# The first three products of a two-request layer on the scaled x, with the share of the norm's shift added as one column for each request

## The chip, the cores and the metric

One core of a Trainium2 chip runs the whole kernel. The metric is the device time of one execution in microseconds (us); lower is better. Profiles are of one execution, and times in a profile count from the start of its span.

## The reference

One layer of a diffusion backbone is computed for two requests with shared weights: 128 context tokens (request 0) and 512 latent tokens (request 1), 640 in all, of width 1024. What matters here is its start:

```
sh1, sc1, g1, sh2, sc2, g2 = split(silu(c) @ w_mod + b_mod, 6)    # one set for each request
h  = rmsnorm(x, norm_g[0]) * (1 + sc1) + sh1
z  = h @ w_in                       # 1024 x 7200
zx, zg, q, k, v, g, lr, ga, gb = split(z)
xc = conv_centred(zx, conv_w, conv_b)          # per row of the grid, for request 1
hf, hb = rg_lru_scan(xc, ...)                  # forward and backward
```

After that come the gated linear attention, two gated up-projections, `w_out`, a second norm and a squared-ReLU MLP. With `a1 = norm_g[0] * (1 + sc1)` the first norm's output is `xn * a1 + sh1`, where `xn` is x divided by its root mean square, and so `h @ w = (xn * a1) @ w + sh1 @ w`. The last term is the same for all tokens of a request.

## The kernel before

Activations lie transposed, features on the 128 partitions and the 640 tokens along the free axis, as 8 tiles of 128 features (k = 0 to 7). A product of h with a weight is made exact enough by splitting both operands into a rounded high part and a low part: weight pieces are `whi` and `wlo`, h is `HH` and `HL`, and each k gives three terms (whi x HH, whi x HL, wlo x HH), each in two halves of 320 tokens. So one output piece of 128 features (a unit) takes 8 x 3 x 2 = 48 matmuls.

**The order of the work.** All operations go into a recorder in program order (`Recorder.add`, with their dependences). `Recorder.order` then simulates the engines with costs of its own and, whenever an engine is free, takes the operation with the lowest index that is ready by its simulation (casts of weights count as 50 places earlier). Each engine issues its own list in that order and does not pass over a waiting instruction. Tiles come from pools: 43 tiles `t` in SBUF, 4 `whi` and 4 `wlo`, 2 raw weight buffers, and in PSUM 2 `dense` and 2 `aux` tiles. A tile is given out of turn only if the tiles that are due before it can still be had. All instructions are issued on line 343, so the profile's groups are told apart by their tiles.

**The start.** The SP queue loads x, and `EARLY` and `MIX` give the order of the rest: `m` in `EARLY` and `l` in `MIX` are loads of `w_mod` (`mod_load`, four DMAs of 256 KB for 256 columns, scale and shift columns in turn, 8 loads in all), `d` and `D` loads of `w_in`, `x` the transposes of a tile of x, `p` the splits of the first weight pieces, `m` in `MIX` a pair (`mod_pair`) and `h` two tiles of h (`make_h`).

`mod_pair(n)` multiplies silu(c) with the scale and the shift columns of tiles 2n and 2n+1. Each product has 32 output rows (two are used), and four of them write four groups of 32 partitions of one `aux` tile. ACT copies the result to `rw`, and products with `sel` add the four groups and turn them into columns, which DVE writes to `a1` and `sh1`. `make_h(k)` scales and shifts tile k (DVE does request 0, ACT request 1), DVE rounds it into `HH` and subtracts for `HL`.

**The first unit.** `first_part(k)` makes tile k of the first three pieces of zx at once (`first_ps`: two `dense`, one `aux`), as soon as `HH` and `HL` of that k are there. `first_post` then calls `post_zx` for each: DVE copies request 0 and ACT request 1 out of PSUM to a padded tile `zp`, and both compute the convolution, from which the LRU chains start (gates on `aux` tiles, tanh, exp, sqrt, scans). The fourth piece, zx3, needs a `dense` tile again, and the units of zx, lr, q, k, v, g and zg follow, all on `HH` and `HL`.

Of the kernel before, what the change touches and what calls it, by code (L numbers as in the profile page):

```python
# [21 lines left out]
GR = 8  # L22
# [15 lines left out]
MH_ENG = "VAVV"  # L38
# [4 lines left out]

EARLY = "xxxrxxmm"
MIX = "XdllxxxxxDllmphllmhmhmh"
N_FIRST = 3


# [341 lines left out]
def tile_hybrid_layer(  # L392
# [8 lines left out]
    V, A, PE, G, SP = (Port(rec, e) for e in ("DVE", "ACT", "PE", "POOL", "SP"))  # L401
# [25 lines left out]
    def flat(ps):  # L427
        return ps.rearrange("p a b -> p (a b)")
# [7 lines left out]
    f32 = lambda ap: ap.bitcast(F32)  # L436
    act = A.activation
    by = {"A": A, "V": V, "G": G}

    def copy(e, dst, src):  # L440
        A.copy(dst, src) if e == "A" else by[e].tensor_copy(dst, src)

    def scaled(e, dst, src, scale, bias):

        if e == "A":
            act(dst, src, AF.Copy if bias is None else AF.Identity, scale=scale, **({} if bias is None else {"bias": bias}))
        else:
            by[e].tensor_scalar(dst, src, scale, bias, op0=OP.mult, **({} if bias is None else {"op1": OP.add}))
# [43 lines left out]
    wm = w_mod[0]  # L492
    wm_r = wm.rearrange("(k p) n -> p k n", p=128)

    def mod_load(m):

        c0 = D * (1 - m % 2) + 256 * (m // 2)
        parts = [t_("modw")[:, 0:512].rearrange("p (k n) -> p k n", k=2) for _ in range(4)]
        for i, p in enumerate(parts):
            SP.dma_start(out=p, in_=wm_r[:, 2 * i:2 * i + 2, c0:c0 + 256])  # L500
        return parts

    def x_load(t):
        a, b = t_(f"xa{t}"), t_(f"xb{t}")
# [2 lines left out]
        SP.dma_start(out=b[:, 0:512], in_=src[..., 512:1024])  # L507
        xin.append((a, b))

    xin, modw = [], []  # L510
    for s_ in EARLY:
        if s_ == "r":
            load_rows(rows_mod, SP)
        elif s_ == "m":
            modw.append(mod_load(len(modw)))
        else:
            x_load(len(xin))


    ps = aux()  # L520
# [17 lines left out]
    cst32 = consts.tile([128, 8, 32], F32, name="cst32")  # L538
# [3 lines left out]
    ps = aux()  # L542
# [6 lines left out]
    sel = consts.tile([128, 2], F32, name="sel")  # L549
# [68 lines left out]
    cols = {}  # L618
    for nm in ("a1", "sh1", "a2", "sh2"):
        cols[nm] = consts.tile([128, 2, 8], F32, name=nm)  # L620
    bm1 = consts.tile([128, 8], F32, name="bm1")
# [7 lines left out]
        for e, x in zip(XN_ENG, xin[t]):  # L629
            scaled(e, x[:, 0:512], x[:, 0:512], q, None)  # L630

    def mod_pair(n):


        ps = aux()

        for m in (1, 0):
            for r in (1, 0):
                for j in (3, 2, 1, 0):
                    k = 4 * r + j  # L640
                    PE.matmul(ps[32 * j:32 * (j + 1), m, 0:256], cst32[:, k, :], modw[2 * n + m][k // 2][:, k % 2, :],
                              start=r == 1, stop=r == 0)
        rw = t_("rw")
        A.copy(rw[:, 0:512].rearrange("p (m c) -> p m c", m=2), ps[:, :, 0:256])
        for m in range(2):
            for i in range(2):
                k = 2 * n + i
                pc = ps[:, m, 256 + 2 * i:258 + 2 * i]
                PE.matmul(pc, rw[:, 256 * m + 128 * i:256 * m + 128 * (i + 1)], sel, start=True, stop=True)
                if m:  # L650
                    V.tensor_scalar(cols["sh1"][:, :, k], pc, bm(0, k), None, op0=OP.add)
                else:
                    V.tensor_scalar(cols["a1"][:, :, k], pc, bm1[:, k:k + 1], ng(0, k), op0=OP.add, op1=OP.mult)

    xnT = []
    HH = rec.tile(big, 1, [128, 8, T], F32R, "HH", "hh")
    HL = rec.tile(big, 1, [128, 8, T], F32R, "HL", "hl")

    def x_T(t, ps):
        for k in range(KT):  # L660
            PE.transpose(flat(ps)[:, 128 * k:128 * (k + 1)], xin[t][k // 4][:, 128 * (k % 4):128 * (k % 4 + 1)], ident)
        for k in range(KT):
            copy(XT_ENG[t], xnT[k][:, 128 * t:128 * (t + 1)], flat(ps)[:, 128 * k:128 * (k + 1)])

    def make_h(k):
# [42 lines left out]
    def startup():  # L708
        ps = aux()
        PE.transpose(ps[:, 0, 0:80], v2[0:80, :], ident[0:80, 0:80])  # L710
        V.tensor_copy(C2, ps[:, 0, 0:80])
        V.tensor_scalar(bm1, bmv(1), 1.0, None, op0=OP.add)
        for t in range(NT):
            x_norm(t)
        load_rows(rows_etc, G)
        ps = aux()
        PE.transpose(ps[:, 0, 0:114], v1[0:114, :], ident[0:114, 0:114])
        V.tensor_copy(C1, ps[:, 0, 0:114])
        nm = nx = nh = 0
        for s_ in MIX:  # L720
            if s_ == "l":
                modw.append(mod_load(len(modw)))
            elif s_ == "m":
                mod_pair(nm)
                nm += 1
            elif s_ == "X":
                xnT.extend(t_(f"xnT{k}") for k in range(KT))
            elif s_ == "p":
                prep(0, 0, 0)
            elif s_ == "h":  # L730
                for k in (2 * nh, 2 * nh + 1):
                    make_h(k)
                nh += 1
            elif s_ in "dD":
                do_loads(1 if s_ == "d" else 2)
            else:
                x_T(nx, dense())
                nx += 1


    def fm_mm(ps, piece, xh, xl, c0, c1, ks, k_all=KT):

        w = (c1 - c0) // 2 if c1 - c0 > 512 else c1 - c0
        wh = piece.hi.rearrange("p (k m) -> p k m", k=KT)
        terms = [(wh, xh), (wh, xl)]
        if piece.lo is not None:
            terms.append((piece.lo.rearrange("p (k m) -> p k m", k=KT), xh))
        for k in ks:
            for n, (ww, xx) in enumerate(terms):
                for j in range((c1 - c0) // w):  # L750
# [36 lines left out]

        return t[:, base:base + 528].rearrange("p (r c) -> p r c", c=66)[:, :, 0:64]

    def post_zx(ps, f):  # L790
# [4 lines left out]
        V.tensor_copy(z[:, 1:129], ps[:, 0, 0:128])  # L795
        A.copy(zr[:, :, 1:25], ps[:, 0, 128:320].rearrange("p (c r) -> p r c", r=GR))
        A.copy(zr[:, :, 25:65], ps[:, 1, 0:320].rearrange("p (c r) -> p r c", r=GR))
# [19 lines left out]
    def first_post():  # L817
        for u in range(N_FIRST):
            post_zx(first_ps[u], u)
# [949 lines left out]
    st = {"p": 0, "l": 0}  # L1769
# [73 lines left out]
```

## Time and profile before

| | |
|---|---|
| three timed runs | 1137.08, 1138.93, 1140.58 us; median 1138.93 |
| the profiled execution | 1140.71 us, of which its span is 1138.8 us |
| TensorE (PE) busy in the span | 1109.5 us (97%) |
| VectorE (DVE) busy | 848.1 us (74%) |
| ScalarE (ACT) busy | 616.1 us (54%) |
| granted TensorE clock, mean of the span | 0.99 |
| HBM read | 121.61 MB |

PE is the matmuls, PEld the loads of their stationary operand, SPq the queue that issues most DMAs. An instruction on fp32 data shows as two matmuls. A granted clock of 1.00 is the higher of the two levels (2.4 GHz), 0.50 the lower one (1.2 GHz).

### The profile page before, as it was taken

To read this page: it belongs to the slowest core of one execution; us is meant where nothing else is said; L and a number is where in the kernel's file an instruction comes from. 1 tells how busy PE (TensorE), PEld (TensorE's weight loads), DVE (VectorE), ACT (ScalarE), POOL (GpSimd) and SP (SyncE) were. 2 spreads that over 40 slices of the span, in tenths; PEclk is the share of its full clock that TensorE was granted. 3 is DMA by queue.
4 is the path that set the end of the run, shared out by engine and by line. 5 is a ranking of instruction groups with operands and counts; after the bars stand their busy time and mean duration, and the time that the engine had idled before them with its cause. 6 is when DMAs were issued, how large, how long until landed. Compare 5 with 4: busy or idle time off the path is not lost.

```text
span 1138.8 us, 17811 instructions
## 1 busy us (share of the span) xinstructions
PE 1109.5 (97%) x7020; PEld 1042.9 (92%) x7020; DVE 848.1 (74%) x1363; ACT 616.1 (54%) x998; POOL 78.6 (7%) x152
## 2 busy tenths in 40 slices
PE   6999999999999999999999999999999999999996
PEld 5799898999999999999999988888898899899895
DVE  4686875868474837727996559997779989987767
ACT  5387988895475748611433358744444433333442
POOL 3135103000000000000000011000000000000001
PEclk9999999999999999999999999999999999999998
DMA  9835426251221212227544456422233333222422
GB/s 293 265 74 150 122 66 173 56 163 38 94 75 56 75 57 74 75 74 232 195 157 167 130 184 207 145 75 74 74 123 122 110 118 137 95 75 74 154 88 93
DMA packets 104476, 136.94 MB, mean 120 GB/s; under 512 B 8179, under 2 KB 78021, under 8 KB 104393
## 3 DMA queue, kind: packets, MB, share of 16 engines
q1 hardware_dynamic: 102344, 133.91, 37.8%
q0 software_dynamic: 2048, 1.90, 0.7%
q8 instruction: 55, 0.90, 0.3%
q14 instruction: 29, 0.23, 0.1%
HBM read 121.61 MB, written 6.31 MB: 112 GB/s over the span
## 4 chain that ended last, share of the span: by engine, by line
PE 77%; DVE 9%; ACT 6%; DMA 4%; issue 3%; POOL 0%; SPq 0%; DVEq 0%; POOLq 0%; ACTq 0%
PE dense L343 52%; PE aux L343 25%; DVE i L343 3%; DVE th L343 2%; DMA modw<-in_w_mod_dram 1%; DVE wlo L343 1%; ACT r L343 1%; DMA i<-r 1%; ACT L343 1%; ACT th L343 1%; DMA r<-r 1%; DMA raw<-in_w_in_dram 1%; DMA w2raw<-in_gla_w_dram 1%; ACT whi L343 1%; ACT L342 1%
## 5 line engine op out<-in xcount | busy, mean ns | idle before, releaser
L343 ACT CAST whi<-raw 128x1024 fp32r<-128x1024 f32 (+2 forms) x173 | 167.1, 970 | 289.3 <-PE dense L343 141.5
L343 DVE TENSOR_TENSOR wlo<-raw,whi 128x1024 fp32r<-128x1024 f32 (+1 forms) x168 | 190.1, 1133 | 75.8 <-ACT whi L343 75.0
L343 PE MATMUL dense<-HH,whi 128*128 128x320 f32 x768 | 179.0, 313 | 0.5 <-DVE g L343 0.3
L343 PE MATMUL dense<-HL,whi 128*128 128x320 f32 x768 | 176.5, 310 | 0.0
L343 PE MATMUL dense<-HH,wlo 128*128 128x320 f32 x752 | 172.8, 310 | 0.0
L343 PEld LDWEIGHTS dense<-HH,whi 128*128 128x128 f32 x768 | 129.2, 189 | 2.6 <-issue 0.8
L343 PEld LDWEIGHTS dense<-HL,whi 128*128 128x128 f32 x768 | 129.4, 189 | 0.0
L343 PEld LDWEIGHTS dense<-HH,wlo 128*128 128x128 f32 x752 | 126.4, 189 | 0.0
L343 PE MATMUL dense<-whi,ah 128*128 128x512 f32 (+1 forms) x288 | 113.0, 392 | 0.0
L343 PE MATMUL dense<-wlo,ah 128*128 128x512 f32 (+1 forms) x288 | 113.0, 392 | 0.0
L343 PE MATMUL dense<-whi,al 128*128 128x512 f32 (+1 forms) x288 | 113.0, 392 | 0.0
L343 DVE SCALAR_TENSOR_TENSOR mac<-mw,cst,mac 128x512 f32<-128x512 f32 x112 | 78.1, 746 | 0.0
L343 PE MATMUL aux<-H2H,whi 128*128 128x320 f32 (+1 forms) x240 | 74.8, 311 | 0.0
L343 PE MATMUL aux<-H2L,whi 128*128 128x320 f32 (+1 forms) x240 | 74.7, 311 | 0.0
L343 PE MATMUL aux<-H2H,wlo 128*128 128x320 f32 (+1 forms) x240 | 74.6, 311 | 0.0
L343 PEld LDWEIGHTS dense<-whi,al 128*128 128x128 f32 x288 | 54.1, 188 | 12.5
L343 PEld LDWEIGHTS dense<-whi,ah 128*128 128x128 f32 x288 | 54.1, 188 | 10.3
L343 PEld LDWEIGHTS dense<-wlo,ah 128*128 128x128 f32 x288 | 54.1, 188 | 10.2
L343 ACT CAST whi<-s 128x512 fp32r<-128x512 f32 x42 | 26.0, 619 | 67.1 <-PE aux L343 62.9
L343 PE MATMUL aux<-f,whi 128*128 128x320 f32 x224 | 59.4, 308 | 0.0
L343 DVE TENSOR_TENSOR fa<-fa,dense 128x512 f32<-128x512 f32 x66 | 45.2, 686 | 17.8 <-PE dense L343 17.6
L343 PE MATMUL aux<-f,wlo 128*128 128x320 f32 x168 | 51.9, 309 | 0.0
(335 smaller groups left out, 2500.1 us busy)
## 6 DMA issues: line engine op xcount, KB each, us to landing
raw<-in_mlp_w_dram SPq DMA_DIRECT2D x34, 1024.0 KB, 5.0
raw<-in_w_in_dram SPq DMA_DIRECT2D x24, 1024.0 KB, 5.3
mw<-in_w_mod_dram SPq DMA_DIRECT2D x64, 256.0 KB, 5.4
modw<-in_w_mod_dram SPq DMA_DIRECT2D x32, 256.0 KB, 5.9
raw<-in_w_out_dram SPq DMA_DIRECT2D x8, 1024.0 KB, 4.8
i<-r SPq DMA_DIRECT2D x32, 160.0 KB, 2.4
raw<-in_w_in_dram SPq DMA_DIRECT2D x8, 512.0 KB, 4.6
raw<-in_lru_up_dram SPq DMA_DIRECT2D x4, 1024.0 KB, 4.9
```

What stands on the lines that cost most here:

```text
L342: nc.scalar.preload_act_table_set("natural_log_exp_and_others")
L343: getattr(eng[o.eng], o.name)(*o.args, **o.kw)
```

## The change

The loads of `w_mod` are sorted: the four for the scale come first, then the four for the shift (`mod_load(part)`). `mod_pair(part, n)` handles one of the two. `make_h1(k)` scales tile k and splits it into `h1h` and `h1l`, 16 tiles of the pool; the first unit multiplies these, and not `HH` and `HL`. `make_h(k)` adds the shift later, in place of the former scaling and shifting, and gives `HH` and `HL` for all other products. `first_bias` multiplies sh1 with the three weight pieces (48 products with 32 output rows and 128 columns), turns the result into columns `zb`, and `post_zx` adds them on the way out of PSUM.

```diff
-EARLY = "xxxrxxmm"
-MIX = "XdllxxxxxDllmphllmhmhmh"
+EARLY = "xxxrxxss"
+MIX = "XdsDsxxxxxmphttmhmhttmhMHMHMHMH"
...
-    def mod_load(m):
+    def mod_load(part):
...
-    def mod_pair(n):
+    def mod_pair(part, n):
         ps = aux()
-        for m in (1, 0):
-            for r in (1, 0):
-                for j in (3, 2, 1, 0):
...
+        for r in (1, 0):
+            for j in (3, 2, 1, 0):
+                k = 4 * r + j
+                PE.matmul(ps[32 * j:32 * (j + 1), 0, 0:256], cst32[:, k, :], modw[part][n][k // 2][:, k % 2, :],
+                          start=r == 1, stop=r == 0)
         rw = t_("rw")
-        A.copy(rw[:, 0:512].rearrange("p (m c) -> p m c", m=2), ps[:, :, 0:256])
...
+        A.copy(rw[:, 0:256], ps[:, 0, 0:256])
+        for i in range(2):
+            k = 2 * n + i
+            pc = ps[:, 0, 256 + 2 * i:258 + 2 * i]
+            PE.matmul(pc, rw[:, 128 * i:128 * (i + 1)], sel, start=True, stop=True)
...
+    def make_h1(k):
+        x = xnT[k]
+        for e, (i, sl) in zip(MH_ENG, requests):
+            scaled(e, x[:, sl], x[:, sl], cols["a1"][:, i, k:k + 1], None)
+        hi, lo = t_("h1h", F32R), t_("h1l", F32R)
+        copy(MH_ENG[2], hi[:, 0:T], x[:, 0:T])
+        by[MH_ENG[3]].tensor_tensor(lo[:, 0:T], x[:, 0:T], f32(hi[:, 0:T]), op=OP.subtract)
+        h1.append((hi, lo))
+
     def make_h(k):
         x = xnT[k]
-        for e, i, sl in zip(MH_ENG, range(2), (slice(0, 128), slice(128, T))):
-            scaled(e, x[:, sl], x[:, sl], cols["a1"][:, i, k:k + 1], cols["sh1"][:, i, k:k + 1])
-        copy(MH_ENG[2], HH[:, k, :], x[:, 0:T])
-        by[MH_ENG[3]].tensor_tensor(HL[:, k, :], x[:, 0:T], f32(HH[:, k, :]), op=OP.subtract)
+        for e, (i, sl) in zip(MH_ENG, requests):
+            sh = cols["sh1"][:, i, k:k + 1]
+            if e == "A":
+                act(HH[:, k, sl], x[:, sl], AF.Identity, bias=sh)
+            else:
+                by[e].tensor_scalar(HH[:, k, sl], x[:, sl], sh, None, op0=OP.add)
+        for i, sl in requests:
+            V.scalar_tensor_tensor(HL[:, k, sl], x[:, sl], cols["sh1"][:, i, k:k + 1], f32(HH[:, k, sl]), op0=OP.add,
+                                   op1=OP.subtract)
...
+    def post_zx(ps, f, b=None):
...
+            if b is None:
+                copy("A" if n else "V", dst, src)
+            elif n:
+                act(dst, src, AF.Identity, bias=b[:, 1:2])
+            else:
+                V.tensor_scalar(dst, src, b[:, 0:1], None, op0=OP.add)
...
     def first_part(k):
         if k == 0:
             first_ps.extend([dense(), dense(), aux()])
+        if k == KT - 2:
+            first_bias()
         for u, p in enumerate(pzx[0:N_FIRST]):
-            fm_mm(first_ps[u], p, hh, hl, 0, T, (k,))
+            fm_mm(first_ps[u], p, lambda k: h1[k][0], lambda k: h1[k][1], 0, T, (k,))
+
+    def first_bias():
+        sh32 = t_("sh32")[:, 0:256].rearrange("p (k i) -> p k i", k=KT)
+        G.memset(sh32, 0.0)
+        V.tensor_copy(sh32[:, :, 0:2], cols["sh1"].rearrange("p i k -> p k i"))
+        ps, rw, b = aux(), t_("rw"), sm_("zb")
+        for u, p in enumerate(pzx[0:N_FIRST]):
+            for n, w in enumerate((p.hi, p.lo)):
+                for r in (0, 1):
+                    for j in range(4):
+                        k = 4 * r + j
+                        PE.matmul(ps[32 * j:32 * (j + 1), 0, 128 * u:128 * (u + 1)], sh32[:, k, :],
+                                  f32(w)[:, 128 * k:128 * (k + 1)], start=n == 0 and r == 0, stop=n == 1 and r == 1)
+        A.copy(rw[:, 0:128 * N_FIRST], ps[:, 0, 0:128 * N_FIRST])
+        for u in range(N_FIRST):
+            PE.matmul(ps[:, 1, 2 * u:2 * u + 2], rw[:, 128 * u:128 * (u + 1)], sel, start=True, stop=True)
+        V.tensor_copy(b[:, 0:2 * N_FIRST], ps[:, 1, 0:2 * N_FIRST])
+        first_ps.append(b)
```

In `MIX`, `s` and `t` now load scale and shift columns, `m` and `M` are a scale and a shift pair, `h` and `H` are `make_h1` and `make_h` for two tiles.

## Rows read from the trace of the kernel before

**Rows 1.** Windows: stretch and its length, each engine's busy time, clock, DMA share, GB/s.

```profile
33.10:62.30 29.20, 29.13 (x237) 26.36 (x234) 17.22 (x36) 11.08 (x17) 8.79 (x17) 0.99 0.68 209
62.30:100.00 37.70, 37.70 (x259) 37.70 (x258) 32.46 (x49) 28.48 (x46) 18.37 (x45) 1.00 0.53 127
...
120.00:125.00 5.00, 3.16 (x14) 2.90 (x13) 5.00 (x9) 3.79 (x5) 0.00 (x0) 0.75 0.34 80
```

**Rows 2.** Chain that ended last, 0 to 130 us: start, length, what.

```profile
22.62 6.91 DMA modw<-in_w_mod_dram
29.57 3.64 PE aux L343 x32
...
62.38 10.56 PE dense L343 x72
```

**Rows 3.** Timeline of PE, 33 to 62 us: start, length, instruction.

```profile
33.14 0.83 PE L343 MATMUL dense<-HH,whi 128*128 128x320 f32 x2
...
41.61 0.28 PE L343 MATMUL aux<-sel,rw 128*128 128x2 f32 x2
41.75 0.39 PE L343 MATMUL dense<-HH,whi 128*128 128x320 f32 x1
...
45.23 1.93 PE L343 MATMUL aux<-modw,cst 128*32 128x256 f32 x32
47.10 0.56 PE L343 MATMUL aux<-HL,whi 128*128 128x320 f32 x2
...
53.41 0.46 PE L343 MATMUL aux<-HH,whi 128*128 128x320 f32 x2
...
61.92 0.46 PE L343 MATMUL aux<-HH,wlo 128*128 128x320 f32 x2
```

**Rows 4.** Timeline of ACT, 20 to 65 us, idle time before in brackets.

```profile
20.81 1.45 ACT L343 COPY xnT<-dense 128x128 f32<-128x128 f32 x8 [1.63 <-PE dense L343]
22.63 1.99 ACT L343 CAST whi<-raw 128x1024 fp32r<-128x1024 f32 x2 [0.36 <-DMA raw<-in_w_in_dram]
24.52 0.58 ACT L343 COPY rw<-aux 128x512 f32<-128x512 f32 x1
...
61.32 0.65 ACT L343 COPY zp<-dense 128x192 f32<-128x192 f32 x2
```

**Rows 5.** Windows with tile modw alone: stretch, PE, PEld, clock, DMA share, GB/s.

```profile
29.50:33.20 3.70, 3.63 (x32) 1.38 (x32) 0.50 1.10 350
```

**Rows 6.** Instructions on tile modw, 9 to 12 us: duration ns, issue times.

```profile
L343 SPq DMA_DIRECT2D modw<-in_w_mod_dram x5: 397/467/468, 9.0 to 11.5; - x5
```

**Rows 7.** The same view, 32 to 39 us, with the times to landing.

```profile
L343 SPq DMA_DIRECT2D modw<-in_w_mod_dram x9: 368/368/368, 32.6 to 38.5; - x9
...
DMA to landing us min/median/max: 5.8/5.8/5.9
```

**Rows 8.** Timeline of DVE, 48 to 70 us.

```profile
48.93 0.27 DVE L343 TENSOR_SCALAR a<-aux,bm,C 128x2 f32<-128x2 f32 x1
...
66.68 1.01 DVE L343 SCALAR_TENSOR_TENSOR xc<-zp,C,cv 128x128 f32<-128x128 f32 x2
```

**Rows 9.** Groups by form, 0 to 62.4 us: count, busy us, mean ns, idle before.

```profile
L343 DVE TENSOR_TENSOR HL<-xnT,HH 128x640 fp32r<-128x640 f32 x8 | 6.6, 824 | 0.2
L343 ACT ACTIVATE xnT<-xnT,sh,a 128x512 f32<-128x512 f32 x8 | 6.5, 815 | 11.0 <-DVE sh L343 11.0
...
L343 DVE TENSOR_TENSOR wlo<-raw,whi 128x1024 fp32r<-128x1024 f32 x5 | 6.0, 1224 | 5.0 <-ACT whi L343 4.9
...
L343 DVE CAST HH<-xnT 128x640 fp32r<-128x640 f32 x8 | 4.0, 503 | 0.0
...
L343 DVE TENSOR_SCALAR xnT<-xnT,a,sh 128x128 f32<-128x128 f32 x8 | 2.9, 368 | 0.3
```

**Rows 10.** Timeline of PEld around the last block, idle time before it in brackets.

```profile
45.23 1.45 PEld L343 LDWEIGHTS aux<-modw,cst 128*32 128x32 f32 x32 [0.19 <-issue]
47.09 0.30 PEld L343 LDWEIGHTS aux<-HL,whi 128*128 128x128 f32 x2 [0.41 <-issue]
```

More of the change, by code (lines that the diff above doesn't have):

```diff
@@ L493, in tile_hybrid_layer @@
     wm_r = wm.rearrange("(k p) n -> p k n", p=128)
-    def mod_load(m):
-        c0 = D * (1 - m % 2) + 256 * (m // 2)
-        parts = [t_("modw")[:, 0:512].rearrange("p (k n) -> p k n", k=2) for _ in range(4)]
-        for i, p in enumerate(parts):
+    def mod_load(part):
+        c0 = D * part + 256 * len(modw[part])
+        bufs = [t_("modw")[:, 0:512].rearrange("p (k n) -> p k n", k=2) for _ in range(4)]
+        for i, p in enumerate(bufs):
             SP.dma_start(out=p, in_=wm_r[:, 2 * i:2 * i + 2, c0:c0 + 256])
-        return parts
+        modw[part].append(bufs)
     def x_load(t):
@@ L508, in x_load @@
         xin.append((a, b))
-    xin, modw = [], []
+    xin, modw = [], ([], [])
     for s_ in EARLY:
@@ L513, in tile_hybrid_layer @@
             load_rows(rows_mod, SP)
-        elif s_ == "m":
-            modw.append(mod_load(len(modw)))
+        elif s_ == "s":
+            mod_load(1)
         else:
@@ L630, in x_norm @@
             scaled(e, x[:, 0:512], x[:, 0:512], q, None)
-    def mod_pair(n):
+    def mod_pair(part, n):
         ps = aux()
-        for m in (1, 0):
-            for r in (1, 0):
-                for j in (3, 2, 1, 0):
-                    k = 4 * r + j
-                    PE.matmul(ps[32 * j:32 * (j + 1), m, 0:256], cst32[:, k, :], modw[2 * n + m][k // 2][:, k % 2, :],
-                              start=r == 1, stop=r == 0)
-        rw = t_("rw")
-        A.copy(rw[:, 0:512].rearrange("p (m c) -> p m c", m=2), ps[:, :, 0:256])
[L645 to L653, printed above, removed]
+        for r in (1, 0):
[3 more added lines that the diff above has]
+                          start=r == 1, stop=r == 0)
+        rw = t_("rw")
+        A.copy(rw[:, 0:256], ps[:, 0, 0:256])
[3 more added lines that the diff above has]
+            PE.matmul(pc, rw[:, 128 * i:128 * (i + 1)], sel, start=True, stop=True)
+            if part:
+                V.tensor_scalar(cols["a1"][:, :, k], pc, bm1[:, k:k + 1], ng(0, k), op0=OP.add, op1=OP.mult)
+            else:
+                V.tensor_scalar(cols["sh1"][:, :, k], pc, bm(0, k), None, op0=OP.add)
     xnT = []
@@ L663, in x_T @@
             copy(XT_ENG[t], xnT[k][:, 128 * t:128 * (t + 1)], flat(ps)[:, 128 * k:128 * (k + 1)])
+    requests = ((0, slice(0, 128)), (1, slice(128, T)))
+    h1 = []
+    def make_h1(k):
[6 more added lines that the diff above has]
+        h1.append((hi, lo))
     def make_h(k):
         x = xnT[k]
[L667 to L670 removed]
+        for e, (i, sl) in zip(MH_ENG, requests):
[7 more added lines that the diff above has]
+                                   op1=OP.subtract)
     bdr = consts.tile([128, 2, 2, 128], F32, name="bdr")
@@ L718, in startup @@
         V.tensor_copy(C1, ps[:, 0, 0:114])
-        nm = nx = nh = 0
+        n = dict.fromkeys("xmMhH", 0)
         for s_ in MIX:
[L721 to L725, printed above, removed]
+            if s_ in "st":
+                mod_load(1 if s_ == "s" else 0)
+            elif s_ in "mM":
+                mod_pair(1 if s_ == "m" else 0, n[s_])
+            elif s_ in "hH":
+                for k in (2 * n[s_], 2 * n[s_] + 1):
+                    (make_h1 if s_ == "h" else make_h)(k)
             elif s_ == "X":
@@ L729, in startup @@
                 prep(0, 0, 0)
[L730 to L733, printed above, removed]
             elif s_ in "dD":
                 do_loads(1 if s_ == "d" else 2)
-            else:
-                x_T(nx, dense())
-                nx += 1
+            elif s_ == "x":
+                x_T(n[s_], dense())
+            if s_ in n:
+                n[s_] += 1
     def fm_mm(ps, piece, xh, xl, c0, c1, ks, k_all=KT):
@@ L794, in post_zx @@
         zr = z[:, 130:658].rearrange("p (r c) -> p r c", c=66)
-        V.tensor_copy(z[:, 1:129], ps[:, 0, 0:128])
-        A.copy(zr[:, :, 1:25], ps[:, 0, 128:320].rearrange("p (c r) -> p r c", r=GR))
-        A.copy(zr[:, :, 25:65], ps[:, 1, 0:320].rearrange("p (c r) -> p r c", r=GR))
+        parts = ((z[:, 1:129], ps[:, 0, 0:128]), (zr[:, :, 1:25], ps[:, 0, 128:320].rearrange("p (c r) -> p r c", r=GR)),
+                 (zr[:, :, 25:65], ps[:, 1, 0:320].rearrange("p (c r) -> p r c", r=GR)))
+        for n, (dst, src) in enumerate(parts):
+            if b is None:
+                copy("A" if n else "V", dst, src)
+            elif n:
+                act(dst, src, AF.Identity, bias=b[:, 1:2])
+            else:
+                V.tensor_scalar(dst, src, b[:, 0:1], None, op0=OP.add)
         tmp = t_("cv")
@@ L813, in first_part @@
             first_ps.extend([dense(), dense(), aux()])
+        if k == KT - 2:
+            first_bias()
         for u, p in enumerate(pzx[0:N_FIRST]):
-            fm_mm(first_ps[u], p, hh, hl, 0, T, (k,))
+            fm_mm(first_ps[u], p, lambda k: h1[k][0], lambda k: h1[k][1], 0, T, (k,))
[16 more added lines that the diff above has]
+        first_ps.append(b)
     def first_post():
+        b = first_ps[N_FIRST]
         for u in range(N_FIRST):
-            post_zx(first_ps[u], u)
+            post_zx(first_ps[u], u, b[:, 2 * u:2 * u + 2])
             posted.add(f"zx{u}")
```

1 line of the change is left out of this document (removed).

## The prediction

> **What bounds the kernel now.** The page's busy times come first: PE is busy for 97% of the span, so time is won only where PE idles or does less. The windows of the start say where that is: from 33.1 to 62.3 us PE is busy for 29.13 of 29.20 us, while DVE works for 17.22 and ACT for 11.08 [rows 1]. The chain of waits shows what lies ahead of that. It goes through the loads of the modulation weights to 29.53 us (22.62 + 6.91), then through the second pair's products, 3.64 us long, and from there through PE without a gap worth naming to the fourth piece at 62.38 [rows 2]. So two numbers decide the start: when the first products begin, now 33.14 [rows 3], and how much PE work lies between them and the fourth piece. I call the start of the fourth piece T; it is 62.38 now. From 62.3 to 100 us PE is busy without a break, so I take a shift of T as a shift of the end; a stretch where PE idles is 120 to 125 us, 1.84 of 5 us [rows 1].
>
> PE's 29.24 us from 33.14 to 62.38 split as follows. A product of 320 columns follows the last one after 0.1467 us: from 53.41 to 61.92 there are 29 steps of two, 8.51 / 58 [rows 3]. The 144 products of the first unit take 21.12. The third and fourth pair lie in that stretch; a block of 16 products takes 1.87 from its start to the next product (45.23 to 47.10), two take 3.74 [rows 3]. A `sel` product, two instructions, moves the next one by 0.14 (41.61 to 41.75); twelve make 1.68 [rows 3]. The rest, 29.24 - 26.54 = 2.70, is short waits and the first products at the lower clock: the second pair just ahead ran at a granted clock of 0.50 [rows 5].
>
> **When the first products begin.** The first scaled tile now needs one load of 1 MB instead of two. The first five of its DMAs were issued by 11.5 us [rows 6], and a landing takes about 5.8 [rows 7], so the first scale columns can be made from about 17.3 us, while x is still being transposed. ACT ends its last eight copies of x at 22.26, and the first raw weights are there at 22.63 [rows 4]. If both scalings of the first pair (0.815 each [rows 9]) go next, ACT is at 23.9, the first weight cast (half of 1.99 [rows 4]) ends at 24.9, the second at 25.9, and DVE's first `wlo` (1.224 [rows 9]) at 26.1. The first product can start at 24.9, a steady stream at about 26. If `rw` stays behind the two casts as now (24.52 [rows 4]), the column needs at most 1.8 more, the time from the end of the fourth pair's block (47.1 [rows 3]) to its first column (48.93 [rows 8]), and 0.27 itself; then come 0.815 and a rounding of 0.503 [rows 9]: 27.9. I take 26.0, with bounds 24.9 and 27.9, so 7.1 us earlier than now.
>
> **What PE does more.** (1) The blocks. A pair is now two blocks of 8 products. Behind the start lie six of them: the last scale pairs and the four shift pairs. A half of 1.87 is 0.94 from below. From above, the weight loads stand still for 0.19 before a block and 0.41 behind it [rows 10]; if all 0.60 is paid by each block, it is 1.27 / 2 + 0.60 = 1.24. I take 1.1, six make 6.6 (5.6 to 7.4), against 3.74 now. (2) The `sel` products of the pairs stay 16 in all, 12 behind the start, 1.68; three are added for the bias, 0.42. (3) The bias: 48 products in the same form as a block, with 128 columns in place of 256. By columns one costs 1.87 / 16 / 2 = 0.058, 2.8 in all; by count 1.87 / 16 = 0.117, 5.6 in all. Nearer lies the row of the weight loads, 32 in 1.45 us [rows 10]: 96 of them take 4.35 at most, and they can partly overlap. I take 3.5 (2.8 to 5.6). (4) The rest stays at 2.70 (1.7 to 4.5; more if the early products come in drips and keep the clock low).
>
> In the Trainium skill, TensorEngine Tiling (Array Packing), section Key Properties, it says that changing the tiling mode drains TensorE. That speaks against twice as many blocks, and the trace agrees as far as it goes, with those 0.19 and 0.41 us. By the rule alone the sum would take the upper 7.4 for the blocks and end 0.8 later; by the rows alone it stays open how much of the 0.60 is paid once for each block.
>
> **Sum.** 26.0 + 21.12 + 6.6 + 1.68 + 0.42 + 3.5 + 2.70 = 62.0 for T, 0.4 earlier than now. The 7.1 us are almost eaten by 2.9 of blocks moved behind the start and 3.9 for the bias.
>
> **What hides the rest.** On DVE a tile's scaling, rounding and subtraction take 0.368 + 0.503 + 0.824 = 1.70 as now [rows 9]. The later shift adds, for each tile, about 0.37 for request 0's part of `HH` and 1.01 for the two subtractions with an added scalar (nearest row: the convolution's 128 and 512 columns together [rows 8]), 1.38, in all 11.0. Now DVE is free for 12.0 of the 29.2 us [rows 1], and the first tiles start 7 us earlier, so this lies beside PE. On ACT it adds 8 x 0.815 = 6.5 [rows 9] to 11.08. Should the cover fail, it costs what I work out in the third rival. SP issues the same 32 loads in the same number of bytes; the last lands at 38.5 + 5.9 = 44.4 as now [rows 7], and the bdr and raw loads behind it stay. POOL gets one memset, of which only the bias has need. The third of the first pieces still waits for an `aux` tile until the last pairs have theirs, as now (first one shortly before 45.23 [rows 3]); until then PE has 96 products of the two others, 14.1, and five blocks, enough for 26 to 44.
>
> **What comes behind T.** Now ACT empties the first piece from 61.32 [rows 4]. Afterwards two pieces can be finished in the forties, and they wait only for the bias. From the last load at 44.4 its column is ready after a block (1.1) and 1.8 (47.1 to 48.93 [rows 3, 8]), with the second column at about 48; the bias products end by about 54, and 1.8 later the pieces are emptied, some 5 us earlier than now. The LRU chain can start earlier by a part of that, and may take some of the 1.84 us at 120 to 125. I take 1.0 (0 to 1.84).
>
> Together 1.4 us less: 1140.71 - 1.4 = 1139.3 for an execution like the profiled one. That one lies 1.78 above the median of the three runs, so the median goes from 1138.93 to 1137.5. The three differ by 3.5 us; below 0.3%, 3.4 us, I call no change.
>
> **Rivals.** *Faster* (0.31): all terms at their favourable ends, because the recorder's list puts the scalings first and DVE keeps up: 24.9 + 21.12 + 5.6 + 1.68 + 0.42 + 2.8 + 1.7 = 58.2, 4.2 earlier, and 1.8 behind T: 1132.9. For it speaks that ACT idles for 11.0 us before its scalings now [rows 9]; against it, that PE's own extra work is certain.
>
> *No gain, because PE waits in front of the loads* (0.06): PE does not pass over a block whose load is late; the second pair did so and took 3.64 in place of 1.87 [rows 2, 3]. If each of the four shift blocks stood so in front of products that are ready, 4 x 1.77 = 7.1 would come on top, and the time would be 1144.6. Against it: the blocks at 38 and 45 us did not wait, and the shift loads land at the rate at which blocks are used.
>
> *Slower, through the new wait for the bias* (0.15): the fourth piece needs a `dense` tile, and that is free only when the bias column is there. Behind the start of the copy into `sh32`, at X, come 3.5 of products, 1.8 to the column and about 0.9 to empty a piece (0.65 for ACT's two copies [rows 4]): T is at least X + 6.2. It decides from X = 55.8 on, and it is slower by 3.4 from X = 59.6. If DVE reaches the last two scaled tiles (3.4) and all eight shifted ones (11.0) only at 48, X is 62.4 and T 68.6, which gives 1145.2; with two thirds of that backlog, 57.6 and 63.8, it gives 1140.4. Against it: DVE's work would have to pile up although it is free for 12 us.
>
> **Chances and range.** The forecast has 0.48. Faster by over 0.3%: 0.31. Within: 0.48. Slower: 0.21, the second and third rival. The forecast's own range is 1135.5 to 1142.3; to the faster case the range must reach 1132.5, and to the slower ones 1143.5, which leaves out about 2 in 10.
>
> **What would show it.** The first `dense` product on `h1h` at 26 (24.9 to 27.9); blocks of 16 instructions at about 1.1; bias instructions, 96, at 3.5 in all; the fourth piece at 62.0. A DVE copy to `sh32` later than 55.8 with PE idle behind it means the third rival; idle PE in front of blocks on `modw` between 30 and 45 the second. The prediction is wrong if the start moves by less than 5 us, if the bias costs over 5 us, or if the order behind 62 us changes so that PE idles where it does not now.

## The result and the profile after

The changed kernel took 1147.41 us (median of 4, 1145.63 to 1148.33), the kernel before 1139.70 (4 runs): a ratio of 1.008, 95% interval 1.0063 to 1.0097. A second set of runs gave 1144.24 (4 runs) against 1138.49 (25 runs): 1.0055, 1.0036 to 1.0073. It is slower by 0.5 to 0.8%; I had forecast 1137.5 and no change. The profiled execution took 1145.63, its span 1143.7. It is the fastest of its four, while that of the kernel before (1140.71) is slower than any of its timed runs; so the two profiles show 4.9 us of a difference that is 7.7 by the medians.

T, the start of the fourth piece, is 67.18 us by the timeline of PE; 62.0 was forecast. In the kernel before it is 62.21 by the same view:

```profile
62.21 0.46 PE L343 MATMUL dense<-HH,whi 128*128 128x320 f32 x2
```

The 62.38 of the chain [rows 2] counts only from the end of the product ahead. From here on T is that of the timeline in every run.

The first lines of the page, busy times:

```profile
PE 1113.8 (97%) x7122; PEld 1044.8 (91%) x7122; DVE 854.6 (75%) x1389; ACT 626.2 (55%) x1015; POOL 81.0 (7%) x153
```

PE has 102 matmuls more and is busy for 4.3 us longer; that is all the page says. The timeline of PE answers to [rows 3]: start, length, instruction, in brackets the idle time before it and what ended it.

```profile
26.38 1.07 PE L343 MATMUL aux<-modw,cst 128*32 128x256 f32 x16 [0.60 <-DVE a L343]
27.38 0.56 PE L343 MATMUL dense<-h1h,whi 128*128 128x320 f32 x2
...
32.19 1.94 PE L343 MATMUL aux<-modw,cst 128*32 128x256 f32 x16 [1.26 <-DVE h1l L343]
...
35.85 1.94 PE L343 MATMUL aux<-modw,cst 128*32 128x256 f32 x16
...
47.86 1.07 PE L343 MATMUL aux<-modw,cst 128*32 128x256 f32 x16
48.86 0.41 PE L343 MATMUL dense<-h1h,whi 128*128 128x320 f32 x1
...
57.44 0.65 PE L343 MATMUL aux<-whi,sh 128*32 128x128 f32 x16
...
60.20 0.56 PE L343 MATMUL dense<-h1h,whi 128*128 128x320 f32 x2
...
65.95 0.45 PE L343 MATMUL aux<-h1h,wlo 128*128 128x320 f32 x2
67.18 0.56 PE L343 MATMUL dense<-HH,whi 128*128 128x320 f32 x2 [0.78 <-ACT zp L343]
...
115.47 0.56 PE L343 MATMUL dense<-HH,whi 128*128 128x320 f32 x2 [3.42 <-ACT zp L343]
```

The first product comes at 27.38, 5.8 us earlier than before. A half block takes 1.00 (47.86 to 48.86), but 1.87 where the clock is low (32.19 and 35.85). The bias products take 2.76 (57.44 to 60.20). At T PE waits for ACT, which it didn't before. The windows of the same stretch, columns as in [rows 1]:

```profile
27.40:31.60 4.20, 3.09 (x21) 2.39 (x17) 4.20 (x11) 3.50 (x6) 0.31 (x1) 0.99 1.10 348
31.50:38.30 6.80, 6.11 (x40) 3.38 (x41) 5.98 (x12) 2.29 (x5) 0.48 (x6) 0.50 1.09 359
```

From 31.5 to 38.3 us the granted clock is 0.50, the lower level of 1.2 GHz, and PE works for 6.11 of these 6.80 us. In the kernel before there is such a stretch too, and PE is busy for 5.35 us of it:

```profile
26.92:33.75 6.83, 5.35 (x38) 2.99 (x39) 3.70 (x10) 2.81 (x4) 0.00 (x0) 0.50 1.09 347
```

Most of that is the second pair's block, 3.64 us in place of 1.87 [rows 2, 3]. There it cost next to nothing, because PE would have been held up anyway: a `sel` product at 34.15 needs `rw`, and ACT copies that behind a cast whose raw weights came at 32.5:

```profile
32.56 1.05 ACT L343 CAST whi<-raw 128x1024 fp32r<-128x1024 f32 x1 [2.85 <-DMA raw<-in_w_in_dram]
33.51 0.58 ACT L343 COPY rw<-aux 128x512 f32<-128x512 f32 x1
```

A second execution of the kernel before (e11 below) shows it. Its low stretch ends earlier, its first product comes at 32.91 in place of 33.14, and then PE waits for `rw`; T is 62.22, the same:

```profile
34.33 0.38 PE L343 MATMUL aux<-sel,rw 128*128 128x2 f32 x2 [0.56 <-ACT rw L343]
```

In the changed kernel PE waits for a load once behind its start. The bracket at 32.19 names DVE, but the block there multiplies the fourth scale load, whose last part was issued at 25.0 and landed 7.1 later (the view of tile modw, 25 to 25.5 us):

```profile
L343 SPq DMA_DIRECT2D modw<-in_w_mod_dram x1: 652/652/652, 25.0 to 25.0; - x1
...
DMA to landing us min/median/max: 7.1/7.1/7.1
```

In a second execution (e7 below) the bracket names the load, and the block starts before DVE's `h1l` has ended:

```profile
32.42 1.93 PE L343 MATMUL aux<-modw,cst 128*32 128x256 f32 x16 [0.17 <-DMA modw<-in_w_mod_dram]
31.64 0.82 DVE L343 TENSOR_TENSOR h1l<-xnT,h1h 128x640 fp32r<-128x640 f32 x1
```

From 27.4 to 31.6 DVE is busy without a break. Its timeline in the changed kernel says with what:

```profile
23.78 2.35 DVE L343 TENSOR_TENSOR wlo<-raw,whi 128x1024 fp32r<-128x1024 f32 x2
...
26.24 0.48 DVE L343 CAST h1h<-xnT 128x640 fp32r<-128x640 f32 x1
...
55.06 0.21 DVE L343 COPY sh<-sh 128x16 f32<-128x16 f32 x1
...
62.02 0.17 DVE L343 COPY zb<-aux 128x6 f32<-128x6 f32 x1 [6.74 <-PE aux L343]
```

And ACT's:

```profile
22.41 2.05 ACT L343 CAST whi<-raw 128x1024 fp32r<-128x1024 f32 x2
...
24.93 0.41 ACT L343 COPY rw<-aux 128x256 f32<-128x256 f32 x1
...
64.39 2.00 ACT L343 CAST whi<-raw 128x1024 fp32r<-128x1024 f32 x2 [3.06 <-PE dense L343]
66.30 1.15 ACT L343 ACTIVATE zp<-dense,zb 128x192 f32<-128x192 f32 x3
...
95.81 1.55 ACT L343 ACTIVATE th<-r,p4sp 128x640 f32<-128x640 f32 x2 [4.95 <-POOL p4sp L343]
```

The second `rw` stands behind two weight casts, the rounding behind two `wlo`. At 64.39 two more casts, which themselves waited 3.06 us for PE, stand ahead of the emptying of the first piece, although its column was there at 62.2. At 95.81 ACT waits for a constant of the recurrence (`p4sp`), is late from then on, and PE idles at 112.

**Where T went.** With the measured sizes, 27.38 (start) + 21.12 (products, as forecast) + 5 x 1.00 (half blocks) + 13 x 0.14 (`sel`) + 3.63 (bias) + 0.95 (hand-over to the fourth piece, 66.24 to 67.18) = 59.90; the rest to 67.18 is 7.28, where I had put 2.70. The clock makes about 3.1 of it, an estimate: half of the 6.11 us that PE works at 0.50. Two waits of PE make 1.59 (1.26 for the load and 0.33 for DVE), and the other 2.6 are small losses. The kernel before has these too: by the timeline its rest is 62.21 - 33.14 - 26.54 = 2.53, of which 0.28 is the clock. In the second profile of the changed kernel the same sum starts at 27.68, ends at 65.71 and leaves 5.51. Against the kernel before, T moves from 62.21 to 67.18 by -5.76 (start), +1.26 (blocks), +0.14 (`sel`), +4.58 (bias with hand-over) and +4.75 (rest).

### The profile page after: what moved, and what is told of

It reads as the page before. It is cut to its first block, busy times and chain, and to the rows that moved or that the text cites. A ratio compares the mean times of both kernels' runs of the same rounds, so it can differ in the third digit from the quotient of the medians.

```text
span 1143.7 us, 18089 instructions
## 1 busy us (share of the span) xinstructions
PE 1113.8 (97%) x7122; PEld 1044.8 (91%) x7122; DVE 854.6 (75%) x1389; ACT 626.2 (55%) x1015; POOL 81.0 (7%) x153
## 4 chain that ended last, share of the span: by engine, by line
PE 80%; DVE 6%; ACT 5%; issue 3%; DMA 2%; POOL 2%; SPq 1%; DVEq 0%; POOLq 0%; ACTq 0%
PE dense L343 55%; PE aux L343 25%; DVE i L343 1%; DMA modw<-in_w_mod_dram 1%; POOL spp L343 1%; SPq L343 1%; DVE th L343 1%; ACT whi L343 1%; ACT L343 1%; ACT r L343 1%; DVE wlo L343 1%; DMA i<-r 1%; ACT L342 1%; ACT junk L343 0%; ACT th L343 0%
## 5 line engine op out<-in xcount | busy, mean ns | idle before, releaser
L343 PE MATMUL dense<-HH,whi 128*128 128x320 f32 x736 | 170.1, 312 | 4.4 <-ACT zp L343 4.2
L343 PE MATMUL dense<-HL,whi 128*128 128x320 f32 x736 | 168.6, 310 | 0.0
L343 PE MATMUL dense<-HH,wlo 128*128 128x320 f32 x720 | 165.3, 310 | 0.0
L343 PEld LDWEIGHTS dense<-HH,whi 128*128 128x128 f32 x736 | 123.4, 189 | 5.4 <-ACT zp L343 4.7
L343 PEld LDWEIGHTS dense<-HL,whi 128*128 128x128 f32 x736 | 123.7, 189 | 0.0
L343 PEld LDWEIGHTS dense<-HH,wlo 128*128 128x128 f32 x720 | 121.1, 189 | 0.0
L343 PEld LDWEIGHTS dense<-whi,ah 128*128 128x128 f32 x288 | 54.1, 188 | 10.2
```

The source lines that it names most:

```text
L343: getattr(eng[o.eng], o.name)(*o.args, **o.kw)
```

## The experiments

Four theories stood against each other: that the loss is PE's added work with the hand-over (**cost**); that it is work at the low clock (**clock**); that the start is bound by loads and DVE, so that PE waits whatever its clock (**supply**); that the recorder's lists behind T have changed (**order**). All ratios are to the kernel before in the same set of runs. "Behind T" is the span less T.

| run | median us (runs) | ratio, 95% | span | first product | T | behind T |
|---|---|---|---|---|---|---|
| before | 1138.93 (3) | | 1138.8 | 33.14 | 62.21 | 1076.6 |
| changed | 1147.41 (4) | 1.0063 to 1.0097 | 1143.7 | 27.38 | 67.18 | 1076.5 |
| e7_again | 1144.24 (4) | 1.0036 to 1.0073 | 1142.9 | 27.68 | 65.71 | 1077.2 |
| e11_before_again | 1139.93 (10) | 0.9992 to 1.0016 | 1137.0 | 32.91 | 62.22 | 1074.8 |
| e1_no_bias | 1134.00 (7) | 0.9938 to 0.9973 | 1135.1 | 27.37 | 61.13 | 1074.0 |
| e6_bias_unused | 1142.85 (10) | 1.0017 to 1.0046 | 1144.6 | 28.75 | 67.85 | 1076.8 |
| e3_dve_post | 1142.65 (10) | 1.0017 to 1.0042 | 1139.5 | 28.70 | 65.12 | 1074.4 |
| e2_warm | 1148.15 (4) | 1.0050 to 1.0085 | 1146.9 | 30.47 | 68.19 | 1078.7 |
| e5_loads_first | 1146.04 (4) | 1.0032 to 1.0065 | 1144.4 | 29.01 | 66.31 | 1078.1 |
| e12_fill_early | 1139.00 (10) | 0.9997 to 1.0021 | 1138.4 | 28.80 | 65.38 | 1073.0 |
| e4_halves | 1138.98 (10) | 0.9992 to 1.0017 | 1138.2 | 30.68 | 62.38 | 1075.8 |
| e9_softplus_first | 1143.90 (5) | 1.0026 to 1.0060 | 1142.1 | 28.57 | 66.69 | 1075.4 |
| e8_third_HH | 1137.27 (10) | 0.9981 to 1.0003 | 1133.7 | 28.15 | 64.30 | 1069.4 |
| e10_HH_dve | 1136.86 (10) | 0.9966 to 0.9990 | 1134.4 | 27.94 | 64.07 | 1070.3 |

### Both kernels once more

The changed kernel, unaltered (e7_again).

> The changed kernel once more, for a second look at the lower clock. Theory A: a stretch of some 7 us at 0.50 comes again between 26 and 39 us but at another place, and the fourth piece moves with it by 1 to 2 us, to 65.2 to 67.2; the time is 6 to 9 us over that of before. Rival: the stretch is tied to the program, the same place and 67.2.

The kernel before, unaltered (e11_before_again).

> The kernel before, profiled once more, for how much its start varies by itself. If the start of the changed kernel varies (first product 27.4 to 27.7, fourth piece 65.7 to 67.2 in two executions) because the stretch at the lower clock falls on products, the kernel before, whose low stretch lies in the wait for loads, should keep its first product within 33.0 to 33.3 and its fourth piece within 62.1 to 62.7, with 1138 to 1140.5. If loads vary by themselves, its fourth piece moves by over 0.8 as well.

The low stretch of the changed kernel's second execution, columns as above:

```profile
27.80:34.60 6.80, 6.63 (x34) 4.93 (x35) 6.80 (x18) 5.04 (x8) 0.67 (x5) 0.50 1.10 353
```

Here the low stretch comes earlier and costs by the same estimate 3.3. The wait for the load is down to 0.17 and that for DVE is gone, since at the lower clock PE comes later to both; T is 1.47 lower. In the kernel before, T differs by 0.01 between two executions (the timeline of PE in e11):

```profile
62.22 0.46 PE L343 MATMUL dense<-HH,whi 128*128 128x320 f32 x2
```

So the changed start is not only longer but also less steady: how the low stretch falls among products and waits now moves T. Behind T the kernel before varies by 1.8 with one and the same list; smaller differences there I don't read.

### The price of the bias

The bias products, their column and its use taken out (e1_no_bias):

```diff
-        if k == KT - 2:
-            first_bias()
...
-            post_zx(first_ps[u], u, b[:, 2 * u:2 * u + 2])
+            post_zx(first_ps[u], u)
```

> The 48 bias products, their three selections and the added columns are left out, so the first three pieces lack the shift's share; all else is the changed kernel. Theory A (the loss lies ahead of the fourth piece, and is the low clock and the wait in front of the fourth scale load, with the bias as a smaller part): the fourth piece starts at 62.9, that is 67.2 less 2.8 for the bias products, 0.6 for the selections and 0.9 for emptying a piece late, and the time falls by about 4.3 us, to 3 above the kernel before. Theory B (the bias and the wait for its column are the loss): the fourth piece at 60 or earlier and the time at or under that of before. Theory C (the order behind the fourth piece is the loss): the time does not follow the start of the fourth piece.

The column computed as before the edit, but not used in `post_zx` (e6_bias_unused; the second half of that diff alone).

> The bias products, the selections and the copy to the column stay, but the first three pieces are emptied without the column (their share of the shift is left out), so nothing waits for it. Theory A (the bias costs what PE works for it, 2.9 + 0.6 us, and 0.9 for emptying the first piece late): the fourth piece starts 0.9 earlier than in the changed kernel, at about 66.3, and the time lies about 1 below it, some 11 to 12 above the kernel without bias. Theory B (waiting for the column, and the order that follows from it, are most of what the bias costs): the time falls by over 5 and comes near the kernel without bias.

DVE in place of ACT empties request 1 of the first piece (e3_dve_post):

```diff
+            elif n and f == 0:
+                V.tensor_scalar(dst, src, b[:, 1:2], None, op0=OP.add)
             elif n:
                 act(dst, src, AF.Identity, bias=b[:, 1:2])
```

> DVE, idle at that time, empties all of the first piece with its column; ACT, which casts two weights first, does not. Theory A: the fourth piece starts 0.9 earlier, at 66.3, and the time falls by 0.9. Theory B with the bias column as the bound: no change at the fourth piece, because the column comes too late anyway. Theory C: the time moves by something else than the fourth piece does.

PE in e1_no_bias, its last shift block and T:

```profile
46.38 1.07 PE L343 MATMUL aux<-modw,cst 128*32 128x256 f32 x16
...
61.13 0.46 PE L343 MATMUL dense<-HH,whi 128*128 128x320 f32 x2
```

The same in e6_bias_unused, whose profiled execution (1146.88) is the longest of its ten:

```profile
49.47 1.07 PE L343 MATMUL aux<-modw,cst 128*32 128x256 f32 x16
...
67.85 0.46 PE L343 MATMUL dense<-HH,whi 128*128 128x320 f32 x2
```

From the last block to T it is 14.75 without the bias, 18.38 with it unused, and 19.33 in e7_again, whose last block is at 46.38 as well. So the bias costs 3.63 of PE work and 0.95 of hand-over, 4.58 in all. The hand-over is ACT's two casts ahead of `zp`; with DVE emptying the piece it is gone (65.12 - 46.73 = 18.39), and the ratio falls to 1.003.

In e1 T lies between its theories A and B, and the time is B's, under that of the kernel before. Without the bias, T comes 1.1 us earlier than before the change, though the first product comes 5.8 earlier: that is all that is left of the earlier start. The medians say more than T does. By its ratio e1 is 1.0 to 1.2% below the changed kernel, 11 to 14 us, and 0.8% below e6, which lacks the column too and has 3.63 more of PE work ahead of T. So more than half of what e1 gains must lie behind T, as its theory C has it: PE's waits from 70 to 330 us are 4.5 in e1 and 7.2 in e6. The 4.58 is the bias's price at T, not what leaving it out does to the time.

### The clock and the supply

Eight idle products of 128 columns ahead of the third scale block, where PE waits (e2_warm):

```diff
         ps = aux()
+        if part and n == 2:
+            for _ in range(8):
+                PE.matmul(ps[:, 1, 0:128], ident, ident, start=True, stop=True)
```

> Eight idle products of 128 columns (16 instructions, some 1.7 us) stand in front of the third scale pair, where PE idles now between 22.8 and 27.4 us. Theory A: the granted clock stays at 1.00 from 31 to 38 us where it is 0.50 in the changed kernel, and the fourth piece starts about 2.5 earlier, at 64.7; the time falls by the same. Theory B: the added products change nothing or come on top, fourth piece at 67.2 to 68.9.

The fourth scale load ahead of the second load of `w_in` (e5_loads_first):

```diff
-MIX = "XdsDsxxxxxmphttmhmhttmhMHMHMHMH"
+MIX = "XdssDxxxxxmphttmhmhttmhMHMHMHMH"
```

> The second load of w_in goes behind the fourth scale load and not in front of it. Theory A: the fourth scale load lands 3 us earlier, at about 29; the wait of 1.3 us in front of its block and most of the low clock behind it go, and the fourth piece starts at 63.5 to 64.5; the time falls by about 3. Theory B: at most the wait of 1.3 is won, fourth piece at 65.9 or later.

Four idle products behind each of the first two scale blocks (e12_fill_early):

```diff
+        if part and n < 2:
+            for _ in range(4):
+                PE.matmul(ps[:, 1, 0:128], ident, ident, start=True, stop=True)
         rw = t_("rw")
```

> The changed kernel with four idle products of 128 columns behind each of the first two scale blocks, where PE waits 1.42 us for rw anyway (eight in all, about 1.8 us; their results are used by nothing). Unlike the idle products tried ahead of the third block they should not move the first product from 27.4 to 27.7. Theory C (work at the lower clock, 3.3 us of it, is the largest part of what the forecast missed, and the idle time at 23 to 26 us is what lets the clock fall there): the granted clock is 1.00 from 26 to 40, the fourth piece comes 2 to 3.3 us earlier, at 63 to 64.5, and the time is 1140.5 to 1142.5. Theory L (with full clock PE meets the loads and DVE's rounding instead): the clock is 1.00 but PE's waits between 27 and 40 grow by 1.5 to 3 us, the fourth piece stays at 65.5 to 67.5, and the time is 1143.5 to 1147. If the clock falls all the same, the idle products at this place say nothing about its price.

The timeline of PE in e2_warm:

```profile
26.91 1.83 PE L343 MATMUL aux<-ident 128*128 128x128 f32 x14 [0.53 <-DVE a L343]
...
29.47 1.07 PE L343 MATMUL aux<-modw,cst 128*32 128x256 f32 x16
...
33.30 1.02 PE L343 MATMUL aux<-modw,cst 128*32 128x256 f32 x10 [1.97 <-DMA modw<-in_w_mod_dram]
...
34.57 0.63 PE L343 MATMUL aux<-modw,cst 128*32 128x256 f32 x6
...
41.58 1.06 PE L343 MATMUL aux<-modw,cst 128*32 128x256 f32 x14
```

There the clock stayed at 1.00 from 22 us on, yet nothing was won: the idle products moved the first real one to 30.47, and at full speed PE then stood 1.97 in front of the fourth scale load. From the first product to T it took 37.72, and without that wait 35.75, against 38.21 and 37.86 in the changed kernel's two executions without theirs, a difference of 2.1 to 2.5. But e2 has a loss of its own in there: two of its blocks stand in two parts (10 and 6, 2 and 14 instructions), and its five blocks take 6.06 in place of 5.00. It also has one `sel` product fewer there (0.14). With both set right the low stretch costs 3.0 to 3.4 us of PE's time, as by the estimate of half. What the full clock gave back went into the later start and the wait.

Moving the load ahead alone (e5) leaves T at 66.31, as its theory B has it. No wait is left on PE from the first product to T, but the first product comes at 29.01, and the low stretch lasts 10.2 us, with PE at work in it:

```profile
27.00:37.20 10.20, 10.05 (x62) 6.93 (x66) 9.56 (x23) 5.93 (x9) 0.63 (x5) 0.50 1.10 354
```

The second filling (e12) held PE busy for 4.70 of the 5.30 us from 22 to 27.3. The windows of its start:

```profile
22.00:27.30 5.30, 4.70 (x48) 3.47 (x40) 3.18 (x7) 3.96 (x10) 0.00 (x0) 1.00 1.09 349
27.30:31.60 4.30, 3.95 (x26) 2.63 (x26) 4.15 (x9) 3.97 (x7) 0.31 (x1) 0.60 1.10 349
```

The clock fell all the same, the first product came 1.1 to 1.4 later, and T is 65.38. By its expectation it says nothing about the price of the clock. But it took 1139.0, as long as the kernel before. Its gain over the changed kernel lies mostly behind T (1073.0 against 1076.5 and 1077.2) and at the hand-over, where PE doesn't wait: adding eight useless products had given other lists. That is the order theory's case, taken up below.

### Two half blocks for one

The kernel before, with each pair as two half blocks, each with its own copy to `rw` (e4_halves):

```diff
-                mod_pair(nm)
+                mod_pair(1, nm)
+                mod_pair(0, nm)
```

> The kernel before, with each pair as two blocks, the scale's and the shift's, and two copies; loads, order of the pairs and the first products as before. A block of half the products took 1.00 in the changed kernel, a whole one 1.87, so eight halves are 0.5 more than four wholes. Theory A: the fourth piece starts at 62.4 to 63.4 and the time is that of before within 0.2%. Theory D (twice the blocks, with their drains and copies, are a main part of the loss): 2 us or more slower.

A ratio of 1.0005 (0.9992 to 1.0017): the split costs nothing that can be told from the time. The start did not stay as it was, though: the first product comes at 30.68, some 2.3 us earlier than in the kernel before, and PE works for 9.78 of the 10.20 us of a stretch at 0.50 (26.9 to 37.1 us). T is 62.38. So here too products that begin earlier fall into the low clock, and T comes no earlier; what the four further blocks cost alone can't be read from this run.

### The order behind T

The constants of the recurrence at the very start, not tied behind the first unit (e9_softplus_first):

```diff
         V.tensor_copy(C1, ps[:, 0, 0:114])
+        softplus_consts()
...
-        rec.later = rec.ops[-1]
-        softplus_consts()
-        rec.later = None
```

> The changed kernel with the constants of the recurrence (softplus, the chain on POOL that ends in p4sp) emitted right behind the transposed rows at the start, and not tied behind the first unit's last operation. In the changed kernel ACT waits 4.9 us for p4sp in its list at 95 us, and PE idles 3.42 us at 112 for zp, which stands behind on ACT. Theory A (the order behind the fourth piece costs 2 to 3 us by way of that wait): the fourth piece stays at 65.5 to 67.5, PE's wait at 112 to 116 is gone, the first lr tile comes at 114 to 117 in place of 117 to 119.5, and the time is 1141 to 1143. Theory B (the stall is only the place where ACT's backlog shows, whoever is late): PE waits as long elsewhere between 100 and 200, and the time is 1144 to 1147.

The third of the first pieces multiplies `HH` and `HL`, as before the change, and needs no column (e8_third_HH; `first_bias` runs over two pieces):

```diff
         for u, p in enumerate(pzx[0:N_FIRST]):
-            fm_mm(first_ps[u], p, lambda k: h1[k][0], lambda k: h1[k][1], 0, T, (k,))
+            if u == 2:
+                fm_mm(first_ps[u], p, hh, hl, 0, T, (k,))
+            else:
+                fm_mm(first_ps[u], p, lambda k: h1[k][0], lambda k: h1[k][1], 0, T, (k,))
```

> The third piece, whose products begin only at 49 us, multiplies HH and HL again, which are there by then for the first tiles, so the bias is needed for two pieces: 32 products and two selections in place of 48 and three. Theory A: 16 products of 0.058 and a selection of 0.19 go, the fourth piece starts 1.1 earlier and the time falls by 1.1. If the shifted tiles are late (the last at 55 us), PE waits for them and the gain is lost: no change.

That, with the edit of e3_dve_post (e10_HH_dve).

> The changed kernel with two edits that were tried alone: the third piece multiplies HH and HL (its column falls away, 32 products left for the other two), and DVE alone empties the first piece. Theory A (the two losses are separate terms: a third of the bias products, and 0.8 to 0.95 at the hand-over to the fourth piece): the fourth piece at 63.2 to 63.6 in place of 64.3, 1135.5 to 1137, a little below the kernel before. Theory B (the two overlap, since the third piece's other order has already moved ACT's list): the fourth piece at 64.0 to 64.6 and 1136.5 to 1138.5, no difference from the one edit alone.

PE's waits from 70 to 330 us, in us, times and the longest, in the changed kernel (the last row of each list, 0.2 for `vc`, is left out):

```profile
PE dense L343 <- ACT zp L343: 3.4, 1, 3.4
PE aux L343 <- DVE xs L343: 1.7, 1, 1.7
PE aux L343 <- ACT r L343: 1.5, 2, 1.3
PE aux L343 <- DVE la L343: 1.4, 2, 1.1
...
```

In e9_softplus_first:

```profile
PE aux L343 <- DVE xs L343: 2.0, 1, 2.0
PE aux L343 <- ACT r L343: 1.7, 3, 0.7
PE aux L343 <- DVE la L343: 1.5, 1, 1.5
PE dense L343 <- ACT zp L343: 1.0, 1, 1.0
PE aux L343 <- DVE nst L343: 0.7, 1, 0.7
...
```

In e8_third_HH:

```profile
PE dense L343 <- DVE vb L343: 1.4, 1, 1.4
PE aux L343 <- ACT r L343: 1.2, 2, 1.0
PE aux L343 <- DVE ab L343: 0.4, 1, 0.4
...
```

Taking away ACT's wait for `p4sp` took 2.4 from one stall and left 7.1 of 8.2 us in all; the time, 1143.9, is that of e7_again. So the stall at 112 shows a backlog of ACT and DVE, and isn't its cause. Nor is it what the change added: the kernel before waits 7.6 and 7.8 us in the same stretch in its two executions. In e8 the waits are 3.2, and behind T it takes 1069.4, 7 less than the changed kernel: 5.0 are these waits, and 1.6 is the clock, which reads 0.80 in the 8 us around the stall at 112 in the changed kernel and 1.00 in e8. The windows of 112 to 120 us, the changed kernel first:

```profile
112.00:120.00 8.00, 4.58 (x22) 4.53 (x22) 6.24 (x10) 5.94 (x10) 4.64 (x8) 0.80 0.60 176
```

```profile
112.00:120.00 8.00, 8.00 (x56) 8.00 (x56) 3.28 (x4) 7.94 (x11) 0.29 (x1) 1.00 0.42 133
```

e8 takes away a third of the bias products (0.9) and T goes to 64.30; DVE's emptying on top of it (e10) brings 64.07, so the two losses overlap. e10 is the only version with the whole result that beats the kernel before, by 0.2% (0.9966 to 0.9990). Its T is theory B's; its time fits both. Why its lists fit better behind T than the changed kernel's I can't say from these runs: T is 2 us later than before there, and the gain is all behind it.

Of the four theories, cost is shown: 4.58 at T, gone when the bias is taken out. Clock is about 3 us, worked out from rows, with no run that isolates it. Supply is 0.2 to 1.6 us of waits, and it takes up what a full clock gives back. Order adds nothing that shows between the two kernels' profiles, but it moves the variants by as much as 7 us behind T.

## Why the prediction was wrong

- **When the first products begin: a little late, inside its bounds.** 27.38 and 27.68 in place of 26.0 (24.9 to 27.9). The upper bound's case held: `rw` stood behind the two casts and the rounding behind both `wlo`. The second scale pair's block also stood ahead of the first product, which makes it five half blocks behind the start and not six.
- **The blocks: over-priced.** 1.00 each and not 1.1; five make 5.0 in place of 6.6. The Trainium skill, TensorEngine Tiling (Array Packing), section Key Properties, says that a change of the tiling mode drains TensorE. The trace shows how little that is here: half of the pair's 1.87 is 0.94, so a block of its own pays 0.06, and the first product behind a block moves the next by 0.25 in place of 0.147 (48.86 to 49.11). Start and blocks together come to 32.4, forecast 32.6.
- **The bias: its work right, its hand-over left out.** Products 2.76 and all of its PE work 3.63, forecast 3.92 with its three `sel`. The fourth piece then comes 0.95 later, because ACT's list has two casts ahead of `zp`. The third rival had the place right, a wait for the emptied tile, but not the way: the copy to `sh32` started at 55.06, before its threshold of 55.8, and DVE kept up.
- **"The rest stays at 2.70": the step that failed.** It measured 7.28 and 5.51, beyond its bound of 4.5. I had read that the kernel before ran its second pair at a clock of 0.50, and took 2.70 over, although the low stretch cost next to nothing there: PE would have waited for `rw`, behind a late load, in any case. Starting 5.8 us earlier puts products into the stretch without that cover: 3.1 and 3.3 us by the estimate of half, 3.0 to 3.4 by e2_warm. PE's waits, for the fourth scale load and for DVE (1.59 or 0.17), are the other part. The 2.70 itself was misread too. It mixes a start from the timeline with an end from the chain (by the timeline alone it is 2.53), and it is hardly waits, since PE idles 0.07 there [rows 1]: about 1.2 is that the first product behind a `sel` or a block moves the next by 0.23 to 0.25 in place of 0.147. "More if the early products come in drips and keep the clock low" stood in the text without a price.
- **"What hides the rest".** DVE keeps up on the whole, but from 27.4 to 31.6 it is busy throughout, and the 12.0 us of spare time that I counted lay later.
- **Behind T: a gain of 1.0 that didn't come.** It took 1076.5 and 1077.2, the kernel before 1076.6 and 1074.8. The LRU chain does start earlier in ACT's list, at 95.81 in place of 102.27, and there waits 4.95 for `p4sp`. The third sign of being wrong came with it: PE idles 3.42 at 112, where it did not before.
- **"I take a shift of T as a shift of the end"** fits the changed kernel's profiles (T +5.0 and +3.5, span +4.9 and +4.1 over the first profile of the kernel before; +5.9 is e7_again's span over that of e11_before_again, with +3.5 at T). It does not fit the variants: behind T they take 1069.4 to 1078.7, and PE's waits from 70 to 330 us, 3.2 to 8.9, go with that. So how large the loss is, and whether there is one, hangs on the lists that the recorder happened to make; e12_fill_early, with T at 65.38, is no slower than before.
- **The rivals.** "PE waits in front of the loads" had 0.06 and a time, 1144.6, that is close, but that is luck: no shift block waited. The block that did stand in front of its load was the fourth scale block, for 1.26 or 0.17, and not 7.1.

Not settled: the price of the clock by a run that changes nothing else, since neither filling left the start where it was; and what makes one list suit ACT and DVE behind T better than another.

## What to carry to other kernels

A stretch at the lower clock costs nothing as long as a wait behind it would have held the engine up anyway, and it is dear once work is moved out from under that cover: when a start is pulled forward, price the work that lands there at both levels of the clock, and ask whether loads and helpers (here DVE's roundings and ACT's casts) can feed it any earlier. When a bracket names a releaser, compare a second execution before the wait is put down to it. A correction added in front of a hand-over costs its own work and a place in the list of the engine that hands over; find out what stands ahead of it. Where lists come from a planner, compare several variants before a loss of half a per cent is put down to the edit.

## What the runs showed of the hardware that I had not expected

A stretch at 0.50 showed in the start of the changed kernel at different places (27.8 to 34.6 us in one execution, 31.5 to 38.3 in the other), and not where PE had been least busy: it came in e12_fill_early with PE busy for 4.70 of the 5.30 us ahead of it, and it didn't come at all in e2_warm, where PE was busy for 6.01 of 8.50 us from 22.0 to 30.5; each is one execution. The 96 products with 32 output rows and 128 columns took 29 ns each, 2.76 / 96, just half of the 58 that I worked out for 256 columns: with these shapes the columns set the time, and not the count.
